# A delta-rule stage: GpSimd's arithmetic on VectorE, shorter taps, one queue for a ring of loads

## The chip, the cores and the metric

The kernel runs as one launch on one core of a Trainium2 chip. The metric is the device time of the launch in microseconds; the time given is the median of three runs. Names of engines: TensorE (PE in the profile, its weight loads PEld), VectorE (DVE), ScalarE (ACT), GpSimd (POOL), SyncE (SP). A q behind a name (SPq) is the queue of instructions of that engine, from which it also issues its DMAs.

## What is computed

The reference is two transformer blocks in float32 on 256 latent tokens of width 1024, with 256 context tokens beside them in the first block. The first block has a mixer of two linear-attention branches and a mixture of 32 experts; the second has dilated and latent attention and a gated feed-forward part. The change lies in the first branch of the first mixer, the gated delta rule. Its q, k and v are projections that pass a depthwise convolution of three by three taps: the latent tokens are an image of 4 rows by 64 columns, the context a single line.

```python
def depthwise_conv2d(img, w):
    return lax.conv_general_dilated(img, w[:, :, None, :], window_strides=(1, 1), padding='SAME', ...)

def conv_latent(t, conv_w):      # rows = 256 // 64 = 4
    return depthwise_conv2d(t.reshape(b, rows, GRID_W, ch), conv_w).reshape(b, l, ch)

def conv_context(t, conv_w):     # the middle row of taps alone
    return depthwise_conv2d(t[:, None], conv_w[mid:mid + 1])[:, 0]

def gated_delta_chunked(q, k, v, g, beta, s0):
    ...
    qg = q * jnp.exp(g)[..., None]
    ...
```

The conditioning of the first block is `silu(c) @ w_mod + b_mod`, six vectors of 1024.

## The kernel before

`build` runs the stages in this order: `pre` (norm, the first third of the conditioning), `gates`, `gdn` (the delta rule), `gla` (the second branch), `merge`, `moe` (the experts' weights as one stream of loads on SP's queue) and `post` (the second block).

The delta rule works on 8 heads in 4 pairs. `gdn_pair` (L391) first loads six weight tiles of a pair from `w_in` on GpSimd's queue (L399). For each head and each of q, k, v it splits the weight into a high and a low part (`wsplit` L381, `split` L48): ScalarE writes the high part `whi` (L49), and VectorE, or the engine handed in, the low part `wlo` (L50). In the first two pairs the split of v (j == 2) is handed to GpSimd. TensorE makes the projection in three products (`mm3`, L76 to L78) into a bank `pj`.

`conv_silu` (L357) then does the convolution with 128 channels on the partitions. ScalarE copies the latent tokens into `padl`, a tile of 6 rows by 66 columns whose outer ring stays zero (L364), writes the middle tap into `acc` (L365) and copies the context into `padc` (L367). Eight further taps are added to the 4 by 64 latent tokens on VectorE, each one instruction over 256 elements (L372). For k and v, which have context tokens, the two outer taps of the middle row are applied in two steps: ScalarE scales a shifted copy into `cx` (L374), GpSimd adds it to `acc` (L375). ScalarE makes the Tanh `th` (L377) and VectorE the final product (L378). q has 256 tokens, k and v 512 each. That is 24 convolutions, 16 of them with context.

TensorE transposes kT (L424), norms follow (L433, L435), and the pair's matrices are made: GpSimd masks a broadcast of the gates, `e` (affine_select, L481), ScalarE takes Exp (L485), VectorE forms `mt` and `at` (L487, L489), ScalarE writes Exp of the gates into `qg` (L490), and GpSimd multiplies that with qT (L491), 16 times in all. The small blocks of `mt` go through scratch memory on SP's queue: `blkD` (L496), `X` (L501); VectorE solves them in 62 dependent steps (L515, L516); the results come back through `solD` (L521, L522) and `AB` (L527, L529), also on SP's queue. `gdn_levels` and `gdn_scan` follow on TensorE.

`gdn` (L650) places the next pair's preparation before the levels and scan of the present one, and between pairs puts filling work: projections of the output gates (`lat_act`, `tok_proj`), and the second and third group of the conditioning, `mod_steps(1)` and `mod_steps(2)`. One step of `mod_steps` (L149) takes two tiles of 128 by 1024 of `w_mod` from the ring on SP's queue (L161), and TensorE multiplies them (L162). After the eighth step GpSimd clears a tile, loads the bias (L167, L170) and stores the sum (L174). Step group 0 runs in `pre`.

All these weights come through one ring of six tiles of 4 KB per partition, `K.ring` (L104), named `w`: 48 loads of `w_mod` on SP's queue, those of `w_in` on GpSimd's (L399, L754, L767). A load waits until the tile that it takes over has been read.

The source names the engine of every instruction. The order within an engine is fixed when the program is built, by a planner that works with estimated costs, and it isn't the order of the source: in the profile, filling work of the first pass stands among the preparation of the second pair. At run time each engine and each queue goes through its instructions in that order and waits on semaphores.

Of the kernel before, what the change touches and what calls it, by code (L numbers as in the profile page):

```python
# [7 lines left out]
F32 = mybir.dt.float32  # L8
# [3 lines left out]
AF = mybir.ActivationFunctionType  # L12
OP = mybir.AluOpType
PSUM = bass.MemoryType.PSUM
DRAM = bass.MemoryType.DRAM
P = 128
# [80 lines left out]
def pre(K, dbg=None):  # L97
    tc, nc, I = K.tc, K.nc, K.I
# [50 lines left out]
    def mod_steps(g):  # L149


        hold = {}

        def step(k):
            if k == 0:
                hold["ps"] = K.psum.tile([P, 512], F32, name="mod", bufs=1)
            ps = hold["ps"]
            for q in range(4):
                if q % 2 == 0:
                    w = ring.tile([P, 1024], F32, name="w")  # L160
                    nc.sync.dma_start(w, I["w_mod"][0, k * P:(k + 1) * P, g * 2048 + q * 512:g * 2048 + (q + 2) * 512])  # L161
                nc.tensor.matmul(ps[32 * q:32 * q + 32, :], csP[:, k, :], w[:, q % 2 * 512:(q % 2 + 1) * 512],  # L162
                                 start=(k == 0), stop=(k == 7), skip_group_check=True)
            if k < 7:
                return
            brow = K.ring.tile([P, 512], F32, name="w") if g else K.wsp.tile([P, 512], F32, name="la", bufs=2)
            nc.gpsimd.memset(brow, 0.0)  # L167
            bm = I["b_mod"][0, g * 2048:(g + 1) * 2048].rearrange("(q n) -> q n", n=512)
            for r in range(2 if g == 0 else 1):
                nc.gpsimd.dma_start(brow[r:P:32, :], bm)  # L170
            row = brow
            nc.vector.tensor_add(row, ps, brow)
            if g:
                nc.gpsimd.dma_start(K.modD[g - 1].rearrange("(q n) -> q n", n=512), row[0:P:32, :])  # L174
                return
            pt = G()
            for b in range(4):
                nc.tensor.transpose(pt[:, b * P:(b + 1) * P], row[:, b * P:(b + 1) * P], K.ident)
            for r in range(2):
                nc.vector.tensor_copy(K.modT[:, r].rearrange("p h (q b) -> p (h q) b", b=4),  # L180
                                      pt.rearrange("p (b q r) -> p r q b", b=4, r=32)[:, r])
        return [lambda k=k: step(k) for k in range(8)]


# [46 lines left out]
def gates(K, dbg=None):  # L231
# [4 lines left out]
    K.gdn_es = ExitStack()  # L236
    padp = K.gdn_es.enter_context(tc.tile_pool(name="pads", reuse_waits="tile", bufs=1, side="right"))
    for i in range(2):
        pl_ = padp.tile([P, 6, 66], F32, name=f"padl{i}")
        pc_ = padp.tile([P, 258], F32, name=f"padc{i}")  # L240
        nc.vector.memset(pl_, 0.0)
        nc.vector.memset(pc_, 0.0)
        K.pads.append((pl_, pc_))
# [113 lines left out]
def conv_silu(K, src, n_tok, ct, out, eng):  # L357

    nc = K.nc
    pl, pc = K.pads[K.npad % 2]  # L360
    K.npad += 1
    acc = K.gpool.tile([P, 512], F32, name="acc", bufs=2)
    al = acc[:, 0:256].rearrange("p (r w) -> p r w", r=4)
    nc.scalar.activation(pl[:, 1:5, 1:65], src[:, 0:256].rearrange("p (r w) -> p r w", r=4), AF.Copy)  # L364
    nc.scalar.activation(acc[:, :n_tok], src, AF.Copy, scale=K.taps[:, 4 * 24 + ct:4 * 24 + ct + 1])  # L365
    if n_tok > 256:
        nc.scalar.activation(pc[:, 1:257], src[:, 256:512], AF.Copy)  # L367
    cx = K.gpool.tile([P, 256], F32, name="cx")
    for tap in (0, 1, 2, 3, 5, 6, 7, 8):
        dy, dx = tap // 3, tap % 3  # L370
        w = K.taps[:, tap * 24 + ct:tap * 24 + ct + 1]
        eng.scalar_tensor_tensor(al, pl[:, dy:dy + 4, dx:dx + 64], w, al, op0=OP.mult, op1=OP.add)  # L372
        if n_tok > 256 and dy == 1:
            nc.scalar.activation(cx, pc[:, dx:dx + 256], AF.Copy, scale=w)  # L374
            nc.gpsimd.tensor_add(acc[:, 256:512], acc[:, 256:512], cx)  # L375
    th = K.gpool.tile([P, 512], F32, name="th", bufs=2)
    nc.scalar.activation(th[:, :n_tok], acc[:, :n_tok], AF.Tanh, scale=0.5)  # L377
    eng.scalar_tensor_tensor(out, th[:, :n_tok], 1.0, acc[:, :n_tok], op0=OP.add, op1=OP.mult)  # L378
# [12 lines left out]
def gdn_pair(K, pr):  # L391
# [14 lines left out]
    for hh in range(2):  # L406
# [5 lines left out]
        H.kT = gp.tile([P, 512], F32, name="kT", bufs=4)  # L412
        vT = gp.tile([P, 512], F32, name="vT", bufs=1)
        for j, (dst, n) in enumerate(((H.qT, 256), (H.kT, 512), (vT, 512))):

            hi, lo = wsplit(K, ws[hh * 3 + j], P, nc.gpsimd if pr < 2 and j == 2 else None)
            ps = psum.tile([P, 512], F32, name="pj", bufs=2)
            for k in range(8):
                mm3(nc, ps[:, :n], hi[:, k, :], lo[:, k, :], K.hh[:, k, :n], K.hl[:, k, :n], k == 0, k == 7)
            conv_silu(K, ps[:, :n], n, j * 8 + h, dst, nc.vector)  # L420
# [40 lines left out]
    for hh, H in enumerate(heads):  # L461
        h = H.h

        pg = K.G()
        for t in range(4):
            nc.tensor.matmul(pg[:, t * P:(t + 1) * P], H.kT[:, t * P:(t + 1) * P], H.kT[:, t * P:(t + 1) * P],
                             start=(t == 0), stop=(t == 3), skip_group_check=True)
        pq = K.G()
        for t in range(2):
            nc.tensor.matmul(pq[:, t * P:(t + 1) * P], H.kT[:, t * P:(t + 1) * P], H.qT[:, t * P:(t + 1) * P],  # L470
                             start=(t == 0), stop=(t == 1), skip_group_check=True)
        H.at = gp.tile([P, 2, 2, P], F32, name="at", bufs=4)
        H.qg = gp.tile([P, 2, 2, P], F32, name="qg", bufs=4)
        H.mt = mt[:, hh]
        H.mt2 = mt
        for d in range(2):
            gbc = gp.tile([P, 4, P], F32, name="gbc", bufs=2)
            nc.scalar.dma_start(gbc, dap(K.gD, d * 32 * P + h * P, [[0, P], [8 * P, 4], [1, P]]))
            e = gp.tile([P, 4, P], F32, name="e", bufs=2)
            s = 1 if d == 0 else -1  # L480
            nc.gpsimd.affine_select(out=e, in_=gbc, pattern=[[0, 4], [s, P]], compare_op=OP.is_ge,  # L481
                                    fill=-1e30, base=0, channel_multiplier=-s)
            for t in range(4):
                col = d * 32 + t * 8 + h
                nc.scalar.activation(e[:, t, :], e[:, t, :], AF.Exp, bias=K.ngc[:, col:col + 1])  # L485
            for t in range(4):
                nc.vector.scalar_tensor_tensor(H.mt[:, d, t, :], pg[:, t * P:(t + 1) * P], H.d[:, d, t:t + 1],  # L487
                                               e[:, t, :], op0=OP.mult, op1=OP.mult)
            nc.vector.tensor_mul(H.at[:, d], pq[:, 0:256].rearrange("p (t i) -> p t i", t=2), e[:, 0:2, :])  # L489
            nc.scalar.activation(H.qg[:, d], gbc[:, 0:2, :], AF.Exp)  # L490
            nc.gpsimd.tensor_mul(H.qg[:, d], H.qg[:, d], H.qT.rearrange("p (t i) -> p t i", t=2))  # L491
    yield


# [1517 lines left out]
```

## Time and profile before

| what | value |
|---|---|
| time, median of 3 runs | 2084.25 us (2083.65 to 2087.07) |
| the profiled execution's own time | 2083.65 us |
| its span, first to last instruction | 2081.9 us |
| TensorE busy | 1898.8 us (91%) |
| VectorE busy | 965.6 us (46%) |
| ScalarE busy | 652.5 us (31%) |
| GpSimd busy | 184.0 us (9%) |
| mean granted clock of TensorE | 0.954 of full speed |

The delta rule runs from about 60 to 560 us, the expert stream from about 740 to 1700 us. "Busy" is the time in which an engine carries out instructions; waiting and issuing DMAs aren't in it, except that a DMA issued by GpSimd counts as busy time of that engine. A wait is listed with the engine that waited, the line that it waited to run, and the instruction or DMA that ended the wait. The granted clock is the mean share of full speed that TensorE was granted in a stretch, between its two levels of 1.2 and 2.4 GHz.

### The profile page before, as it was taken

To read this page: it belongs to the slowest core of one execution; us is meant where nothing else is said; L and a number is where in the kernel's file an instruction comes from. 1 tells how busy PE (TensorE), PEld (TensorE's weight loads), DVE (VectorE), ACT (ScalarE), POOL (GpSimd) and SP (SyncE) were. 2 spreads that over 40 slices of the span, in tenths; PEclk is the share of its full clock that TensorE was granted. 3 is DMA by queue.
4 is the path that set the end of the run, shared out by engine and by line. 5 is a ranking of instruction groups with operands and counts; after the bars stand their busy time and mean duration, and the time that the engine had idled before them with its cause. 6 is when DMAs were issued, how large, how long until landed. Compare 5 with 4: busy or idle time off the path is not lost. (4 is left out here: it accounts for less than half of the span.)

```text
span 2081.9 us, 27700 instructions
## 1 busy us (share of the span) xinstructions
PE 1898.8 (91%) x10742; PEld 1159.6 (56%) x10743; DVE 965.6 (46%) x2245; ACT 652.5 (31%) x1369; POOL 184.0 (9%) x247
## 2 busy tenths in 40 slices
PE   4796989799998999999999999999999889989998
PEld 1664768687986763333333333333333228779997
DVE  2797785857464641212122221221211137676777
ACT  2553545467554420000000000000000004555554
POOL 1343122211112000000000000000000000000000
PEclk8798999899999989999999999999999988998999
DMA  7347654437544689999999999999999994433551
GB/s 261 77 122 206 183 169 116 112 103 206 169 151 151 254 325 417 417 414 418 417 416 418 418 416 417 418 416 417 418 418 416 417 345 139 140 102 121 183 182 41
DMA packets 191939, 569.60 MB, mean 274 GB/s; under 512 B 47919, under 2 KB 90776, under 8 KB 158650
## 3 DMA queue, kind: packets, MB, share of 16 engines
q1 hardware_dynamic: 160064, 507.19, 63.1%
q0 software_dynamic: 13392, 47.72, 7.4%
q10 hardware_dynamic: 18346, 12.86, 2.5%
q8 instruction: 86, 1.41, 0.3%
q14 instruction: 51, 0.42, 0.1%
HBM read 555.22 MB, written 12.50 MB: 273 GB/s over the span
## 5 line engine op out<-in xcount | busy, mean ns | idle before, releaser
L50 DVE TENSOR_TENSOR wlo<-w,whi 128x1024 fp32r<-128x1024 f32 (+1 forms) x185 | 223.9, 1211 | 132.6 <-ACT whi L49 129.8
L1308 PE MATMUL pg<-w,xT 128*64 128x512 f32 x1024 | 274.4, 605 | 3.5 <-DMA w<-in_w_gu_dram 3.4
L1308 PE MATMUL pl<-w,xT 128*64 128x512 f32 x1024 | 268.1, 593 | 0.0
L49 ACT ACTIVATE whi<-w 128x1024 fp32r<-128x1024 f32 (+1 forms) x189 | 197.3, 1047 | 217.8 <-PE pj L77 70.4
L1330 PE MATMUL po<-w,aT 128*64 128x512 f32 x1024 | 239.9, 608 | 7.1 <-DMA w<-in_w_down_dram 5.7
L1230 ACT ACTIVATE th<-ga 128x512 f32<-128x512 f32 x32 | 20.2, 632 | 613.8 <-DVE ga L1228 613.8
L1338 DVE TENSOR_TENSOR o<-po,g 64x512 f32<-64x512 f32 x64 | 44.1, 689 | 260.1 <-PE po L1330 259.4
L1308 PEld LDWEIGHTS pl<-w,xT 128*64 128x64 f32 x1024 | 75.2, 137 | 146.4 <-issue 146.4
L1330 PEld LDWEIGHTS po<-w,aT 128*64 128x64 f32 x1024 | 69.5, 139 | 141.7 <-issue 121.9
L1308 PEld LDWEIGHTS pg<-w,xT 128*64 128x64 f32 x1024 | 65.2, 136 | 139.4 <-issue 115.9
L1228 DVE TENSOR_SCALAR ga<-pg 128x512 f32<-128x512 f32 x32 | 22.1, 691 | 244.8 <-PE pg L1308 244.8
L77 PE MATMUL pj<-wlo,hh 128*128 128x256 f32 x384 | 116.2, 303 | 2.8 <-DVE wlo L50 2.8
L76 PE MATMUL pj<-whi,hh 128*128 128x256 f32 x384 | 115.2, 300 | 2.9 <-ACT whi L49 2.9
L78 PE MATMUL pj<-whi,hl 128*128 128x256 f32 x384 | 114.6, 299 | 0.0
L76 PE MATMUL pj<-hh,whi 128*128 128x512 f32 (+1 forms) x264 | 100.9, 384 | 12.6 <-ACT hh L49 9.1
L372 DVE SCALAR_TENSOR_TENSOR acc<-padl,taps,acc 128x256 f32<-128x256 f32 x192 | 104.3, 557 | 10.1 <-ACT acc L365 8.0
L78 PE MATMUL pj<-hh,wlo 128*128 128x512 f32 (+1 forms) x264 | 100.0, 380 | 5.9 <-DVE wlo L50 5.7
L77 PE MATMUL pj<-hl,whi 128*128 128x512 f32 (+1 forms) x264 | 100.9, 382 | 0.1
L1288 POOL CAST se<-sel 128x128 fp32r<-128x128 f32 x32 | 22.4, 702 | 828.4 <-PE pl L1292 828.4
L1267 PEld LDWEIGHTS tr<-S,h 128*128 128x128 f32 x480 | 57.9, 191 | 48.6 <-issue 34.9
L77 PEld LDWEIGHTS pj<-wlo,hh 128*128 128x128 f32 x384 | 78.0, 203 | 11.0 <-DVE wlo L50 4.2
L1360 PE MATMUL y<-o,PwT 128*128 128x512 f32 (+1 forms) x136 | 72.2, 641 | 13.0 <-DVE o L1338 10.2
(682 smaller groups left out, 3601.7 us busy)
## 6 DMA issues: line engine op xcount, KB each, us to landing
w<-in_w_gu_dram SPq DMA_DIRECT2D x256, 1024.0 KB, 18.2
w<-in_w_down_dram SPq DMA_DIRECT2D x139, 1024.0 KB, 20.0
w<-in_w_in_dram POOLq DMA_DIRECT2D x72, 512.0 KB, 5.4
w<-in_w_mod_dram SPq DMA_DIRECT2D x48, 512.0 KB, 6.9
w<-in_w_up_dram SPq DMA_DIRECT2D x22, 1024.0 KB, 5.1
w<-in_w_in_dram SPq DMA_DIRECT2D x8, 1024.0 KB, 9.8
gbc<-gD ACTq DMA_DIRECT2D x16, 256.0 KB, 6.2
actD<-la ACTq DMA_DIRECT2D x16, 256.0 KB, 5.0
```

Of the source, the lines that this page charges most:

```text
L49: K.nc.scalar.activation(hi, src, AF.Copy)
L50: (lo_eng or K.nc.vector).tensor_sub(lo, src, hi)
L76: nc.tensor.matmul(out, ah, bh, start=first, stop=False, **kw)
L77: nc.tensor.matmul(out, ah, bl, start=False, stop=False, **kw)
L78: nc.tensor.matmul(out, al, bh, start=False, stop=last, **kw)
L372: eng.scalar_tensor_tensor(al, pl[:, dy:dy + 4, dx:dx + 64], w, al, op0=OP.mult, op1=OP.add)
L1267: nc.tensor.matmul(p[:, kk * P:kk * P + m * CAP], h2[:, t, k * P:(k + 1) * P], S[:, t, e0:e1].rearrange("p e c -> p (e c)"), start=(kk == ...
L1288: nc.gpsimd.tensor_copy(se, sel[:, e, :, None].to_broadcast([P, 2, CAP]))
L1308: nc.tensor.matmul(pp[hs, :], xT[:, k, :], w[:, off + half * 512:off + half * 512 + 512], start=False, stop=(k == 7), skip_group_check=True)
L1330: nc.tensor.matmul(po[dh * CAP:(dh + 1) * CAP, :], aT[:, k % 4, (k // 4) * CAP:(k // 4 + 1) * CAP], w[:, kk * 1024 + dh * 512:kk * 1024 + ...
L1338: nc.vector.tensor_mul(outs[e // 2][e % 2 * CAP:(e % 2 + 1) * CAP, dh * 512:(dh + 1) * 512], po[hs], K.g2[hs])
L1360: nc.tensor.matmul(ps[dh], PwT[g][hs, t, :], outs[g][hs, dh * 512:(dh + 1) * 512], start=(g > 0), stop=True)
```

## The change

Five edits. The w_mod loads of groups 1 and 2 are issued from GpSimd's queue; group 0 stays on SP's. The low half of every weight split is made by VectorE. A tap with dy 0 or 2 runs over the three output rows that have a neighbour in the image, and `padl` loses the two outer rows that it no longer needs. The two outer taps of the context are one VectorE instruction each, as those of the latent tokens are, and `cx` goes. The product of `qg` and qT moves to VectorE. The masks (L481) and the issue of the DMAs stay on GpSimd.

```diff
@@ -158,7 +158,7 @@
             for q in range(4):
                 if q % 2 == 0:
                     w = ring.tile([P, 1024], F32, name="w")
-                    nc.sync.dma_start(w, I["w_mod"][0, k * P:(k + 1) * P, g * 2048 + q * 512:g * 2048 + (q + 2) * 512])
+                    (nc.gpsimd if g else nc.sync).dma_start(w, I["w_mod"][0, k * P:(k + 1) * P, g * 2048 + q * 512:g * 2048 + (q + 2) * 512])
                 nc.tensor.matmul(ps[32 * q:32 * q + 32, :], csP[:, k, :], w[:, q % 2 * 512:(q % 2 + 1) * 512],
                                  start=(k == 0), stop=(k == 7), skip_group_check=True)
             if k < 7:
@@ -236,7 +236,7 @@
     K.gdn_es = ExitStack()
     padp = K.gdn_es.enter_context(tc.tile_pool(name="pads", reuse_waits="tile", bufs=1, side="right"))
     for i in range(2):
-        pl_ = padp.tile([P, 6, 66], F32, name=f"padl{i}")
+        pl_ = padp.tile([P, 4, 66], F32, name=f"padl{i}")
         pc_ = padp.tile([P, 258], F32, name=f"padc{i}")
         nc.vector.memset(pl_, 0.0)
         nc.vector.memset(pc_, 0.0)
@@ -361,18 +361,19 @@
     K.npad += 1
     acc = K.gpool.tile([P, 512], F32, name="acc", bufs=2)
     al = acc[:, 0:256].rearrange("p (r w) -> p r w", r=4)
-    nc.scalar.activation(pl[:, 1:5, 1:65], src[:, 0:256].rearrange("p (r w) -> p r w", r=4), AF.Copy)
+    nc.scalar.activation(pl[:, :, 1:65], src[:, 0:256].rearrange("p (r w) -> p r w", r=4), AF.Copy)
     nc.scalar.activation(acc[:, :n_tok], src, AF.Copy, scale=K.taps[:, 4 * 24 + ct:4 * 24 + ct + 1])
     if n_tok > 256:
         nc.scalar.activation(pc[:, 1:257], src[:, 256:512], AF.Copy)
-    cx = K.gpool.tile([P, 256], F32, name="cx")
     for tap in (0, 1, 2, 3, 5, 6, 7, 8):
         dy, dx = tap // 3, tap % 3
         w = K.taps[:, tap * 24 + ct:tap * 24 + ct + 1]
-        eng.scalar_tensor_tensor(al, pl[:, dy:dy + 4, dx:dx + 64], w, al, op0=OP.mult, op1=OP.add)
+
+        r0, r1 = (1, 0, 0)[dy], (4, 4, 3)[dy]
+        eng.scalar_tensor_tensor(al[:, r0:r1], pl[:, r0 + dy - 1:r1 + dy - 1, dx:dx + 64], w, al[:, r0:r1], op0=OP.mult,
+                                 op1=OP.add)
         if n_tok > 256 and dy == 1:
-            nc.scalar.activation(cx, pc[:, dx:dx + 256], AF.Copy, scale=w)
-            nc.gpsimd.tensor_add(acc[:, 256:512], acc[:, 256:512], cx)
+            eng.scalar_tensor_tensor(acc[:, 256:512], pc[:, dx:dx + 256], w, acc[:, 256:512], op0=OP.mult, op1=OP.add)
     th = K.gpool.tile([P, 512], F32, name="th", bufs=2)
     nc.scalar.activation(th[:, :n_tok], acc[:, :n_tok], AF.Tanh, scale=0.5)
     eng.scalar_tensor_tensor(out, th[:, :n_tok], 1.0, acc[:, :n_tok], op0=OP.add, op1=OP.mult)
@@ -412,8 +413,7 @@
         H.kT = gp.tile([P, 512], F32, name="kT", bufs=4)
         vT = gp.tile([P, 512], F32, name="vT", bufs=1)
         for j, (dst, n) in enumerate(((H.qT, 256), (H.kT, 512), (vT, 512))):
-
-            hi, lo = wsplit(K, ws[hh * 3 + j], P, nc.gpsimd if pr < 2 and j == 2 else None)
+            hi, lo = wsplit(K, ws[hh * 3 + j], P)
             ps = psum.tile([P, 512], F32, name="pj", bufs=2)
             for k in range(8):
                 mm3(nc, ps[:, :n], hi[:, k, :], lo[:, k, :], K.hh[:, k, :n], K.hl[:, k, :n], k == 0, k == 7)
@@ -488,7 +488,7 @@
                                                e[:, t, :], op0=OP.mult, op1=OP.mult)
             nc.vector.tensor_mul(H.at[:, d], pq[:, 0:256].rearrange("p (t i) -> p t i", t=2), e[:, 0:2, :])
             nc.scalar.activation(H.qg[:, d], gbc[:, 0:2, :], AF.Exp)
-            nc.gpsimd.tensor_mul(H.qg[:, d], H.qg[:, d], H.qT.rearrange("p (t i) -> p t i", t=2))
+            nc.vector.tensor_mul(H.qg[:, d], H.qg[:, d], H.qT.rearrange("p (t i) -> p t i", t=2))
     yield
 
 
```

## Rows read from the trace of the kernel before

**Rows 1.** Busy us and instructions by stretch: PE, PEld, DVE, ACT, POOL, clock, DMA, GB/s.

```profile
60.00:560.00 500.00, 434.26 (x3365) 358.75 (x3364) 359.58 (x949) 275.79 (x629) 126.56 (x147) 0.90 0.52 142
740.00:1700.00 960.00, 907.47 (x4063) 336.77 (x4060) 204.25 (x378) 68.78 (x125) 22.36 (x31) 0.99 1.01 412
```

**Rows 2.** Waits of TensorE, 60 to 560 us: us, times, longest.

```profile
PE mod L162 <- DMA w<-in_w_mod_dram: 23.3, 7, 8.3
PE g L424 <- DVE kT L378: 10.2, 4, 3.9
PE g L435 <- ACT th L433: 6.5, 3, 2.5
...
PE pj L78 <- POOL wlo L50: 0.2, 1, 0.2
```

**Rows 3.** The source view of L378: ns least, median, most; idle before it.

```profile
L378 DVE SCALAR_TENSOR_TENSOR qT<-th,acc x8: 412/426/969, 88.3 to 380.2; 128x256 f32<-128x256 f32 x8
L378 DVE SCALAR_TENSOR_TENSOR kT<-th,acc x8: 627/688/1074, 89.5 to 397.5; 128x512 f32<-128x512 f32 x8
...
  ACT th L377: 14.0, 7
```

**Rows 4.** The source view of L372, the latent taps.

```profile
L372 DVE SCALAR_TENSOR_TENSOR acc<-padl,taps,acc x192: 468/484/2619, 77.3 to 405.5; 128x256 f32<-128x256 f32 x192
```

**Rows 5.** Groups by line and form, VectorE, 57 to 560 us: busy us, mean ns.

```profile
L372 DVE SCALAR_TENSOR_TENSOR acc<-padl,taps,acc 128x256 f32<-128x256 f32 x192 | 104.3, 557 | 10.1 <-ACT acc L365 8.0
L50 DVE TENSOR_TENSOR wlo<-w,whi 128x1024 fp32r<-128x1024 f32 x58 | 71.2, 1228 | 36.9 <-ACT whi L49 36.9
...
L378 DVE SCALAR_TENSOR_TENSOR qT<-th,acc 128x256 f32<-128x256 f32 x8 | 4.5, 557 | 10.0 <-ACT th L377 10.0
```

**Rows 6.** Groups by line and form, GpSimd, the whole span.

```profile
L375 POOL TENSOR_TENSOR acc<-acc,cx 128x256 f32<-128x256 f32 x32 | 27.9, 872 | 80.9 <-ACT cx L374 76.9 <-DVE acc L372 4.0
...
L399 POOL DMA_DIRECT2D w<-in_w_in_dram x24 | 21.6, 900 | 78.4 <-PE mod L162 42.6 <-DVE taps L255 13.0 <-DVE sc L209 7.5
L491 POOL TENSOR_TENSOR qg<-qg,qT 128x256 f32<-128x256 f32 x16 | 15.2, 954 | 16.2 <-ACT qg L490 13.4 <-DVE qT L378 2.3 <-DVE r L58 0.4
L50 POOL TENSOR_TENSOR wlo<-w,whi 128x1024 fp32r<-128x1024 f32 x4 | 12.3, 3070 | 6.4 <-ACT whi L49 6.2
...
L997 POOL DMA_DIRECT2D gt<-actD x2 | 1.1, 547 | 0.0
```

**Rows 7.** The source view of L843, a product of two tiles.

```profile
L843 DVE TENSOR_TENSOR qg<-qg,qkv x8: 411/418/424, 558.1 to 640.2; 128x256 f32<-128x256 f32 x8
```

**Rows 8.** The source view of L374, the context copies.

```profile
L374 ACT ACTIVATE cx<-padc,taps x32: 492/509/546, 78.8 to 401.4; 128x256 f32<-128x256 f32 x32
```

**Rows 9.** The timeline, 83 to 90 us: start, duration, instruction.

```profile
82.78 2.18 DVE L372 SCALAR_TENSOR_TENSOR acc<-padl,taps,acc 128x256 f32<-128x256 f32 x5
...
85.64 0.73 POOL L375 TENSOR_TENSOR acc<-acc,cx 128x256 f32<-128x256 f32 x1 [0.18 <-ACT cx L374]
...
87.86 0.40 ACT L377 ACTIVATE th<-acc 128x256 f32<-128x256 f32 x1
...
88.29 0.42 DVE L378 SCALAR_TENSOR_TENSOR qT<-th,acc 128x256 f32<-128x256 f32 x1 [3.33 <-ACT th L377]
```

**Rows 10.** The timeline of GpSimd, 137 to 143 us.

```profile
138.22 4.70 POOL L50 TENSOR_TENSOR wlo<-w,whi 128x1024 fp32r<-128x1024 f32 x1 [4.87 <-ACT whi L49]
```

**Rows 11.** Waits of SP's queue, 60 to 420 us: us, times, longest.

```profile
SPq L161 <- PE mod L162: 58.3, 13, 15.0
```

**Rows 12.** The source view of L161, the loads of w_mod.

```profile
L161 SPq DMA_DIRECT2D w<-in_w_mod_dram x48: 327/328/2576, 6.6 to 292.3; - x48
...
DMA to landing us min/median/max: 4.5/6.9/7.9
```

**Rows 13.** The source view of L399, the loads of w_in.

```profile
L399 POOL DMA_DIRECT2D w<-in_w_in_dram x24: 882/892/949, 31.7 to 314.0; - x24
...
DMA to landing us min/median/max: 4.5/6.6/11.5
```

## The prediction, made before the changed kernel was run

> **What bounds the kernel now.** I read the engine times by stretch first. From 740 to 1700 us the expert weights stream in with the DMA engines full (share 1.01, 412 GB/s): nothing in the delta-rule stage can make that stretch shorter, it can only let it begin earlier. The change lies before it, from about 60 to 560 us. There TensorE is busy 434.3 of 500 us, VectorE 359.6, ScalarE 275.8, GpSimd 126.6, at a mean granted clock of 0.90 [rows 1]. So TensorE is the nearest thing to a bound, and what a change in this stretch can give is its idle time, 65.7 us, and some of the clock that is not granted. Next I read what ends TensorE's waits: the conditioning weights (mod, L162) 23.3 us in 7 waits; kT of the convolution (L424) 10.2 in 4; the Tanh-side tile th (L435) 6.5 in 3; GpSimd's own wlo only 0.2 [rows 2]. Two of these the change touches: the convolution's chain (VectorE, ScalarE and GpSimd in turn) and the loads of w_mod.
>
> After 560 us nothing is changed. TensorE's work up to the stream follows in order on the shared buffers, and the stream's loads wait for buffers that this work frees, so I pass a shift at 560 us on to the end whole; if the stream's start did not follow, every number below would shrink towards no change.
>
> **The change part by part.** Busy time of VectorE first.
>
> Taps with dy 0 and 2 lose one row of four: 6 taps in each of 24 convolutions, 144 instructions, 64 elements less. The same operation at 256 and 512 elements takes 426 and 688 ns [rows 3], 1.02 ns per element, so 65 ns each: -9.4 us. Bounds: 0 (if the cost were all fixed) and a quarter of 484 ns [rows 4], -17.4.
>
> The context taps: 32 new instructions of 256 elements, at the 484 ns of the present tap [rows 4]: +15.5 us; at 426 ns [rows 3] 13.6. They lie between the last latent tap and Tanh, so they lengthen a convolution's VectorE part, by 0.97 less 0.39 us.
>
> The weight splits of v in the first two pairs: 4 at 1228 ns [rows 5] in place of 3070 on GpSimd [rows 6]: +4.9 us. The query scaling: 16 multiplies of the very shape that L843 does in 418 ns [rows 7]: +6.7 us. GpSimd loses 27.9 + 15.2 + 12.3 = 55.4 us [rows 6], ScalarE the 32 copies of 509 ns, 16.3 us [rows 8].
>
> Given back is the stretching. The tap's median is 484 ns but its mean 557, its longest 2619 [rows 4, 5]: 192 x 73 = 14.0 us; qT's final instruction has 426 against 557, 8 x 131 = 1.0 [rows 3, 5]. Nothing in a tap's size varies, so I lay the tail to GpSimd's arithmetic beside it. Bounds: 0 back (it is something else) and the 15.0 us whole; I take the whole, because the median is far below the mean, which a few collisions explain and a general slowness does not. Short instructions are probably stretched too; I leave them out.
>
> Sum for VectorE: -9.4 + 15.5 + 4.9 + 6.7 - 15.0 = +2.7 us. At its share of 72% I put **+2 us** on the path.
>
> Now the waits. The tail of a convolution: in the first head VectorE's last tap ends at 84.96, but ScalarE still has a context copy to make, GpSimd's add ends at 86.37, th starts at 87.86 and qT at 88.29 [rows 9]. With all taps on VectorE, th can start when they end. VectorE waits 14.0 us in 7 times for th [rows 3], and TensorE 16.7 us in 7 for kT and th together [rows 2]. Part of this is Tanh's own duration, and the new taps come before it; I take half of VectorE's 14.0: **-7 us**. Bounds 0 and -14.0.
>
> The split on GpSimd: one of the four runs 138.22 to 142.92 [rows 10], with adds and the next mask behind it on that queue. Four splits last 12.3 us there and 4.9 on VectorE; 7.4 less, of which TensorE feels little directly (0.2, [rows 2]). I take **-3 us**, bounds 0 and -7.4.
>
> The shared queue. 32 of the 48 loads of w_mod (those of the second and third group) go from SP's queue to GpSimd's, where the ring's other loads, the masks (affine_select), brow's memset and the bias loads are. What each costs GpSimd is not in the trace; the nearest rows are 547 ns (a load of 4 KB rows, L997) and 900 ns (L399, 512-byte rows) [rows 6]: 17.5 to 28.8 us; I take the first, as w_mod's rows are of 4 KB. It is less than the 55.4 us freed, so GpSimd stays mostly idle and this is hidden; were that cover gone, masks and loads would be late by it. What stands behind a load that waits for its buffer: masks, whose reader is ScalarE's Exp, and the w_in loads, whose readers are the splits. What is gained: w_in loads no longer stand behind adds that wait for ScalarE, and the small SP transfers (blkD, X, solD, AB) no longer behind w_mod. Most waits of these loads on SP are for TensorE to free a buffer, 58.3 us in 13 [rows 11], and no queue changes that: there are six buffers. To landing both kinds of queue take about the same, 6.9 and 6.6 us median [rows 12, 13]. So of the 23.3 us I take **-4**, bounds -23.3 (all gone) and +23.3 (doubled by what is queued ahead).
>
> GpSimd's loads beside a busy VectorE: the 24 issues of L399 last 882 to 949 ns, in a stretch where VectorE is busy 72% [rows 1, 13]. That is even; I see no load held up by VectorE at its issue. The Trainium skill, "SBUF — State Buffer", section "SBUF: two separate sides", says otherwise: loads issued by GpSimd starve while VectorE holds the port pair that the two share, and it puts 620 ns alone against some 3100 ns beside a copy. By that figure 32 loads would be later by an estimated 79 us in all, in place of nothing.
>
> The clock. 0.10 of 500 us is not granted [rows 1], 50 us. About 14 of 65.7 us of idle time go; in proportion that would be 10 us, but TensorE's own idle time is in the 50 and the level also falls elsewhere: **-3 us**, bounds 0 and -10.
>
> Costed at nothing: the smaller pad's memset (two, at the start of gates, with VectorE idle afterwards).
>
> **Sum**: +2 - 7 - 3 - 4 - 3 = -15 us. The profiled execution's own time is 2083.65 us (span 2081.9 and 1.75 around it), so 2068.65; the median of the runs, 2084.25, lies 0.6 above it: **2069 us**. What a measurement of this kernel can tell from no change is 0.2%, 4.2 us.
>
> **The rivals.**
> - All seven waits for w_mod go: -23.3 in place of -4, **2050 us**. For it: w_in loads now stand behind arithmetic on GpSimd, in the same ring. Against: the waits on a freed buffer. Chance 0.10.
> - TensorE covers it: what VectorE and ScalarE gain is taken up because TensorE is busy 87% and its order is fixed; only the two or three largest stalls move, **2082 us**. Chance 0.10.
> - The stretching is not GpSimd's: then the new 17.7 us of VectorE stay, all on the path in its full stretches, +17.7 for +2, which eats the rest: **2085 us**. Against it stands the tail of [rows 4]. Chance 0.04.
> - Head of the queue (slower): on one in-order queue a w_mod load that waits for TensorE holds the masks and the w_in loads behind it; the 58.3 us of such waits were SP's, where little stood behind them. TensorE's waits double: +23.3 for -4, a sum of +12, **2096 us**. It decides once the 13 waits average over the slack of what is behind; at 4.5 us each that is close. Against it: the ring's loads queue in the order in which buffers free. Chance 0.12.
> - Starved loads (slower): each of the 7 waits grows by the difference between the slowest landing on GpSimd's queue and the median on SP's, 11.5 - 6.9 = 4.6 us [rows 12, 13]: +32 for -4, +21, **2105 us**. The even issues speak against it. Chance 0.06. The Trainium skill's section named above is the rule by which it would happen.
>
> **How the numbers follow.** My forecast has 0.58; with the first rival 0.68 for faster. The two near no change give 0.14, the two slower ones 0.18. The range is 2046 to 2088 us: it takes in the first rival and the bounds of the tail, split and clock terms, and leaves out the slower rivals (0.18) and little else.
>
> **What would show it.** The groups by line: taps of two sizes, about 484 and 420 ns, with mean equal to median; no GpSimd arithmetic but masks; 32 loads of w_mod on GpSimd at some 0.55 us. TensorE's idle time from 60 to 560 us some 15 us less, with shorter waits L424 and L435, and the stream's first full slice as much earlier. Wrong: TensorE's waits for w_mod above 23.3 us, masks or w_in late behind a waiting load, a VectorE that is busy over 375 us in the stretch, or a shift at 560 us that the stream swallows.

## The result, and the profile after

The changed kernel takes **2102.51 us** (median of 4 runs, 2098.03 to 2104.36) against 2085.59 (4 runs of the kernel before on the same chip): a ratio of **1.0075, 95% interval 1.0061 to 1.0090**, 15.6 us slower by the ratio (the two medians are 16.9 us apart). Forecast were 2069 us, a range up to 2088, and 0.68 for faster. Its profiled execution has a span of 2101.6 us, 19.7 more than before.

First the stretches, in the columns of [rows 1]:

```profile
60.00:560.00 500.00, 418.59 (x3212) 341.65 (x3211) 331.79 (x980) 251.73 (x575) 89.42 (x119) 0.87 0.50 138
740.00:1700.00 960.00, 909.47 (x4091) 348.62 (x4089) 215.06 (x391) 78.10 (x139) 22.85 (x33) 0.99 1.00 409
```

In the delta rule every engine has become less busy, TensorE too, by 15.7 us, and its granted clock is lower (0.87 for 0.90, nearer to the lower of its two levels). Less work is done in the same 500 us: all engines wait more. TensorE's idle time was to fall by some 15 us; it rose by 15.7, from 65.7 to 81.4. The stream runs as it did.

Then the groups of VectorE and of GpSimd that the change touches, as in [rows 5] and [rows 6]:

```profile
L50 DVE TENSOR_TENSOR wlo<-w,whi 128x1024 fp32r<-128x1024 f32 x60 | 74.1, 1236 | 61.7 <-ACT whi L49 57.6 <-PE pj L78 4.0
L373 DVE SCALAR_TENSOR_TENSOR acc<-padl,taps,acc 128x192 f32<-128x192 f32 x144 | 58.1, 413 | 9.7 <-ACT acc L365 9.1
L373 DVE SCALAR_TENSOR_TENSOR acc<-padl,taps,acc 128x256 f32<-128x256 f32 x48 | 23.0, 480 | 0.2
L376 DVE SCALAR_TENSOR_TENSOR acc<-padc,taps,acc 128x256 f32<-128x256 f32 x32 | 15.3, 479 | 0.0
L491 DVE TENSOR_TENSOR qg<-qg,qT 128x256 f32<-128x256 f32 x16 | 6.8, 423 | 0.0
```

```profile
L161 POOL DMA_DIRECT2D w<-in_w_mod_dram x32 | 17.2, 538 | 104.2 <-PE mod L162 49.4 <-DVE wlo L50 24.0 <-DVE S L642 12.2
```

The prices are those of the forecast: taps of two sizes at 413 and 480 ns, with no tail left (L373, the former L372, has a longest of 490 ns where [rows 4] has 2619), context taps at 479, products at 423, 32 loads at 538. VectorE's idle time ahead of `wlo` is up instead: 61.7 us, for 36.9 in [rows 5].

The waits of TensorE from 60 to 560 us, as in [rows 2]:

```profile
PE mod L162 <- DMA w<-in_w_mod_dram: 16.4, 8, 5.6
PE pj L78 <- DVE wlo L50: 13.9, 3, 11.3
PE sc L556 <- DMA AB<-solD: 11.1, 2, 7.3
PE sc L556 <- DMA gbc<-gD: 9.7, 1, 9.7
PE pj L77 <- DVE wlo L50: 6.8, 4, 3.1
PE g L424 <- DVE kT L379: 6.5, 3, 3.2
PE pj L76 <- ACT whi L49: 3.2, 4, 1.3
PE pj L76 <- ACT padc L367: 3.1, 1, 3.1
PE pj L76 <- ACT acc L365: 2.9, 1, 2.9
```

The waits that the forecast wanted shorter are shorter: `w_mod` 16.4 us for 23.3, `kT` 6.5 for 10.2, and `th`, 6.5 before, is below these rows. Others have come up: 20.7 us for `wlo` (L77 and L78), and 20.8 us at L556, where the levels of a pair begin. Before, these were 8.5 and 5.0:

```profile
PE pj L78 <- DVE wlo L50: 5.7, 1, 5.7
PE sc L556 <- DMA AB<-solD: 5.0, 4, 3.5
PE pj L77 <- DVE wlo L50: 2.8, 3, 1.7
```

At L556 the profile puts 9.7 us down to `gbc`, a broadcast of the gates. L556 doesn't read that tile (its operands are `AB` and `mt`), so this releaser is in doubt; reads of the solve's result `AB` were still being issued when that wait ended at 323.1 us.

How far each kernel has got is best read at the first load of the expert weights. Up to there, from 60 us, the stretch view gives (before ends at 676.7 us, the changed kernel at 700.5):

```profile
60.00:676.70 616.70, 543.20 (x4060) 449.96 (x4059) 431.49 (x1153) 338.47 (x814) 144.79 (x184) 0.92 0.51 147
```

```profile
60.00:700.50 640.50, 548.18 (x4039) 451.33 (x4038) 410.31 (x1199) 324.39 (x782) 112.87 (x164) 0.89 0.49 142
```

So 23.8 us are lost before the stream: TensorE idles 92.3 us (640.50 less 548.18) in place of 73.5, 18.8 more, and takes 5.0 us longer for its work at a lower clock. About 4 us come back later. VectorE is 21 us less busy and ScalarE 14, so neither has become a bound by its work.

Where does it go? The first pair's solve ends at 208.3 us, 12.8 us earlier than before (221.1). The second pair's ends at 303.6 us (303.7 before), the third's at 410.0 for 395.5, and the last store of the delta rule's output is issued at 570.2 for 553.7. The first gain is real, and the stretches after it lose it and more. The third pair's solve begins 11.4 us late (363.1 us for 351.7), and some 14 of the 23.8 us come after the fourth solve, which ends at 503.4 for 493.4.

**What the order did.** The planner has laid out all engines anew. Here is one wait of the changed kernel, in its timeline of VectorE, then of TensorE:

```profile
393.55 0.48 DVE L373 SCALAR_TENSOR_TENSOR acc<-padl,taps,acc 128x256 f32<-128x256 f32 x1
393.94 0.38 DVE L516 TENSOR_TENSOR X<-X,xtmp 128x224 f32<-128x224 f32 x1
394.25 0.16 DVE L70 TENSOR_TENSOR rs_a<-r 128x6 f32<-128x6 f32 x1
394.32 0.48 DVE L373 SCALAR_TENSOR_TENSOR acc<-padl,taps,acc 128x256 f32<-128x256 f32 x1
394.72 0.37 DVE L515 TENSOR_TENSOR xtmp<-L,X 128x208 f32<-128x208 f32 x1
...
403.63 0.42 DVE L373 SCALAR_TENSOR_TENSOR acc<-padl,taps,acc 128x192 f32<-128x192 f32 x1
403.96 0.26 DVE L516 TENSOR_TENSOR X<-X,xtmp 128x96 f32<-128x96 f32 x1
404.13 1.23 DVE L50 TENSOR_TENSOR wlo<-w,whi 128x1024 fp32r<-128x1024 f32 x1
405.26 0.24 DVE L515 TENSOR_TENSOR xtmp<-L,X 128x80 f32<-128x80 f32 x1
```

```profile
393.63 0.46 PE L76 MATMUL pj<-whi,hh 128*128 128x256 f32 x1 [1.26 <-ACT whi L49]
405.41 0.80 PE L78 MATMUL pj<-hh,wlo 128*128 128x512 f32 x1 [11.32 <-DVE wlo L50]
```

TensorE stops at 394.09 for a split. VectorE is not idle in these 10 us; it is full, with taps of the next head, norms and steps of the solve, one after another, and the split has its place behind them, ahead of the step of 80 columns. The same split stands ahead of the step of 208 columns in the order of before, 16 steps earlier. That the order is at fault was at this point an idea only; the runs below test it.

### The profile page after: what moved, and what is told of

It reads as the page before. It is cut to its first block, busy times and chain, and to the rows that moved or that the text cites. A ratio compares the mean times of both kernels' runs of the same rounds, so it can differ in the third digit from the quotient of the medians.

```text
span 2101.6 us, 27624 instructions
## 1 busy us (share of the span) xinstructions
PE 1900.6 (90%) x10742; PEld 1160.7 (55%) x10743; DVE 945.6 (45%) x2297; ACT 639.5 (30%) x1337; POOL 152.0 (7%) x227
## 3 DMA queue, kind: packets, MB, share of 16 engines
q1 hardware_dynamic: 155456, 490.41, 60.2%
## 5 line engine op out<-in xcount | busy, mean ns | idle before, releaser
L50 DVE TENSOR_TENSOR wlo<-w,whi 128x1024 fp32r<-128x1024 f32 (+1 forms) x189 | 229.3, 1214 | 164.3 <-ACT whi L49 157.4
L77 PE MATMUL pj<-wlo,hh 128*128 128x256 f32 x384 | 114.9, 299 | 6.8 <-DVE wlo L50 6.8
L78 PE MATMUL pj<-hh,wlo 128*128 128x512 f32 (+1 forms) x264 | 103.4, 393 | 14.2 <-DVE wlo L50 14.2
L78 PE MATMUL pj<-whi,hl 128*128 128x256 f32 x384 | 113.1, 295 | 0.0
L77 PE MATMUL pj<-hl,whi 128*128 128x512 f32 (+1 forms) x264 | 101.7, 385 | 0.1
L1360 PE MATMUL y<-o,PwT 128*128 128x512 f32 (+1 forms) x136 | 71.6, 635 | 14.3 <-DVE o L1338 10.2
L373 DVE SCALAR_TENSOR_TENSOR acc<-padl,taps,acc 128x192 f32<-128x192 f32 (+1 forms) x192 | 79.5, 429 | 9.9 <-ACT acc L365 9.1
L77 PEld LDWEIGHTS pj<-wlo,hh 128*128 128x128 f32 x384 | 77.3, 201 | 10.1 <-DVE wlo L50 8.6
L76 PEld LDWEIGHTS pj<-whi,hh 128*128 128x128 f32 x384 | 76.9, 200 | 9.8 <-ACT whi L49 6.1
```

What stands on the lines that cost most here:

```text
L50: (lo_eng or K.nc.vector).tensor_sub(lo, src, hi)
L76: nc.tensor.matmul(out, ah, bh, start=first, stop=False, **kw)
L77: nc.tensor.matmul(out, ah, bl, start=False, stop=False, **kw)
L78: nc.tensor.matmul(out, al, bh, start=False, stop=last, **kw)
L373: eng.scalar_tensor_tensor(al[:, r0:r1], pl[:, r0 + dy - 1:r1 + dy - 1, dx:dx + 64], w, al[:, r0:r1], op0=OP.mult, op1=OP.add)
L1360: nc.tensor.matmul(ps[dh], PwT[g][hs, t, :], outs[g][hs, dh * 512:(dh + 1) * 512], start=(g > 0), stop=True)
```

## The experiments

The time of the kernel before is 2085.55 to 2087.92 us in the four groups of runs. Each ratio is against the kernel before on the same chip, with its 95% interval.

### One part alone, the rest laid out by the planner

The first theory was that the shared queue costs the time (A), the second that any edit makes the planner choose a new order, which costs it (B), the third that VectorE's added work does (C).

The queue edit alone, on the kernel before:

```diff
-                    nc.sync.dma_start(w, I["w_mod"][...])
+                    (nc.gpsimd if g else nc.sync).dma_start(w, I["w_mod"][...])
```

> The kernel before with the queue edit alone: the 32 loads of w_mod on GpSimd's queue, all else as it was. Theory A (the shared queue costs the time: on SP's queue the loads of w_mod stood in line with the small transfers solD and AB, on GpSimd's they run beside them): some 2100 to 2105 us, and the time from the end of a solve to the first matmul of the levels (L556) grows from 7 to 11 us to 13 us or more. Theory B (any edit that moves costs makes the planner lay out another order, and the loss is what that order happens to bring together): no rule for the time, anything from 2070 to 2105 us; but slow solves-to-levels only where four or more loads of the ring are issued between them. Theory C (VectorE's added work costs the time): 2085 us, no change.

Measured 2096.96 us, 1.0051 (1.0025 to 1.0077): a little below A's range, well above C's, within B's.

The whole change without the queue edit:

```diff
-                    (nc.gpsimd if g else nc.sync).dma_start(w, I["w_mod"][...])
+                    nc.sync.dma_start(w, I["w_mod"][...])
```

> The changed kernel with the loads of w_mod back on SP's queue; taps, splits and products as in the changed kernel. Theory A: the queue's loss is gone and the arithmetic's gain is left, 2066 to 2075 us. Theory B: between 2070 and 2105 us, with waits for AB again wherever ring loads fall beside it. Theory C: 2100 us as the changed kernel.

Measured 2116.10 us, 1.0157 (1.0109 to 1.0205). Slower still: theory A falls, and the time lies above the ranges of B and C as well.

The shorter taps and the smaller pad alone, on the kernel before:

```diff
-        pl_ = padp.tile([P, 6, 66], F32, name=f"padl{i}")
+        pl_ = padp.tile([P, 4, 66], F32, name=f"padl{i}")
...
-        eng.scalar_tensor_tensor(al, pl[:, dy:dy + 4, dx:dx + 64], w, al, op0=OP.mult, op1=OP.add)
+        r0, r1 = (1, 0, 0)[dy], (4, 4, 3)[dy]
+        eng.scalar_tensor_tensor(al[:, r0:r1], pl[:, r0 + dy - 1:r1 + dy - 1, dx:dx + 64], w, al[:, r0:r1], ...)
```

> The kernel before with the shorter taps alone (three rows of four, the smaller pad): nothing but 144 shorter VectorE instructions, some 9.8 us less of VectorE. A theory in which only costs count: 2078 to 2085 us, never slower. Theory B: the order is laid out anew from the first convolution on, so the time can go either way by 10 us or more; a slower time shows that the order alone can cost that much, since no instruction of this kernel costs more than before.

Measured 2103.70 us, 1.0105 (1.0058 to 1.0152). This is the telling one: the program has the same instructions as before, 144 of them shorter, and it loses 16 us.

The context taps, the splits and the products on VectorE, with whole taps and SP's queue:

```diff
-            nc.scalar.activation(cx, pc[:, dx:dx + 256], AF.Copy, scale=w)
-            nc.gpsimd.tensor_add(acc[:, 256:512], acc[:, 256:512], cx)
+            eng.scalar_tensor_tensor(acc[:, 256:512], pc[:, dx:dx + 256], w, acc[:, 256:512], op0=OP.mult, op1=OP.add)
...
-            hi, lo = wsplit(K, ws[hh * 3 + j], P, nc.gpsimd if pr < 2 and j == 2 else None)
+            hi, lo = wsplit(K, ws[hh * 3 + j], P)
...
-            nc.gpsimd.tensor_mul(H.qg[:, d], H.qg[:, d], ...)
+            nc.vector.tensor_mul(H.qg[:, d], H.qg[:, d], ...)
```

> The kernel before with GpSimd's arithmetic on VectorE alone (context taps, four splits, the query products), whole taps, w_mod on SP's queue. VectorE's stretching is gone (mean of a tap 480 ns). Theory C: slower, 2095 us or more, with VectorE busier by some 10 us. Theory A: 2075 to 2083 us. Theory B: either way, by the waits for AB and wlo.

Measured 2121.21 us, 1.0170 (1.0126 to 1.0214). Up to its first load of the expert weights, at 718.5 us, VectorE is 422.6 us busy, less than the 431.5 of before although it has 52 instructions more, so its busy time doesn't explain the loss. The time is in C's range, its reason isn't. Four edits, four slower kernels, and the parts do not add up to the whole: nothing in these times belongs to one edit. That fits B, but does not show it.

### The same instructions, the order held

The next runs hold the order. At the end of the part that the planner lays out in one piece (all up to the experts), each instruction gets an edge to the one ahead of it in a list for its engine. Such an edge fixes the order of issue alone; nothing waits by it. The lists are read from another kernel's program. In short form:

```diff
+def pin(tc, nc):
+    ins = {i.name: i for i in nc.cur_bb.bb.instructions}
+    for names in ORDER:
+        for prev, name in zip(names, names[1:]):
+            tc.add_manual_dep(ins[name], prev, NO_WAIT, reason="pin")
...
+    pin(tc, nc)
     with tc.If(m > CAP):
```

The shorter taps alone, in the order of before:

> The shorter taps and the smaller pad alone, with each engine's instructions held in exactly the order that the kernel before has (an ordering edge between neighbours of each engine's list, no wait). Theory order (the loss is what the newly planned order brings together): the 16 us that this edit lost beside the kernel before go, and of the 9.4 us that the taps save some part is seen: 0 to 9 us faster than before, ratio 0.9955 to 1.000. Theory cost (the shorter taps cost time by themselves, by their shape or their place): it stays some 16 us slower, ratio 1.005 to 1.0105.

Measured 2079.98 us, **0.9973** (0.9955 to 0.9990). The 16 us are gone and 5.7 are gained. (No run holds the kernel before in its own order; that holding an order costs little by itself is seen from this run.) GpSimd's adds still run beside the taps here, and a tap of 256 elements still takes 562 ns on average:

```profile
L374 DVE SCALAR_TENSOR_TENSOR acc<-padl,taps,acc 128x256 f32<-128x256 f32 x48 | 26.9, 562 | 0.5
```

The kernel before, not an instruction changed, in the order that the planner chose for the shorter taps:

> The kernel before with not one instruction changed, but with each engine's instructions held in the order that was planned for the shorter taps. Theory order: it is as slow as that kernel or a little slower, since its taps are longer: 14 to 26 us slower than before, ratio 1.007 to 1.0125. Theory cost: the time of the kernel before, ratio 0.998 to 1.002.

Measured 2107.89 us, **1.0110** (1.0084 to 1.0137). The order alone costs some 23 us. Its stretch up to the first expert load (702.5 us):

```profile
60.00:702.50 642.50, 546.47 (x4017) 451.14 (x4016) 431.92 (x1143) 337.65 (x809) 139.85 (x183) 0.89 0.49 142
```

VectorE, ScalarE and TensorE are as busy as in the kernel before, within 3.3 us, but the stretch is 25.8 us longer. TensorE idles 96.0 us, at a clock of 0.89: in its sums the picture of the changed kernel, without the change. The waits that make it up are others, those for `kT` above all (10.2 us before):

```profile
PE g L424 <- DVE kT L378: 22.8, 6, 7.0
PE mod L162 <- DMA w<-in_w_mod_dram: 12.9, 3, 7.5
PE pj L78 <- DVE wlo L50: 10.8, 4, 5.0
```

The whole change, in the order of before (the planner places only what changed its engine):

> The whole change, with every instruction that the kernel before also has held in the order of before on its engine; the 32 context taps stand right behind the tap ahead of them, and the planner places only the 4 splits, 16 products and 32 loads that changed their engine. Theory order: the terms of the prediction's sum now add up, 8 to 22 us faster than before, ratio 0.9895 to 0.996. Theory cost (VectorE's added work or the shared queue costs the time whatever the order): 8 to 20 us slower, ratio 1.004 to 1.0095.

Measured 2079.71 us, **0.9970** (0.9951 to 0.9990): faster than before, but less so than the range of the order theory (0.9895 to 0.996).

The same, with the loads of w_mod left on SP's queue:

> As the run with the whole change held in the order of before, but with the loads of w_mod left on SP's queue. It tells what the shared queue is worth at a fixed order. Theory order: 4 us slower than that run (the prediction's term), within a bound of 10 either way; both faster than before. Theory cost by the shared queue: this run is some 15 us faster than that one. Theory cost by VectorE's added work: both are slower than before by 8 to 20 us.

Measured 2074.17 us, **0.9939** (0.9918 to 0.9960). Its first load of the expert weights is issued at 669.5 us:

```profile
60.00:669.50 609.50, 538.07 (x4064) 445.22 (x4063) 416.95 (x1207) 325.60 (x784) 89.64 (x132) 0.93 0.52 149
```

All four runs go the way of theory B, though the whole change gains less than it asked for, and is faster without the shared queue, not slower as expected. That an instruction or the queue costs the 16 us whatever the order falls on all four. Between the profiled executions of before and of this last run the stretch is 7.2 us shorter (the medians differ by 11.6): 2.1 us less idle time of TensorE and 5.1 us less for its work, at a clock of 0.93. Its longest waits for the convolution have become shorter than in [rows 2]:

```profile
PE mod L162 <- DMA w<-in_w_mod_dram: 22.4, 6, 9.0
PE g L424 <- DVE kT L379: 7.9, 3, 3.9
PE sc L556 <- DMA AB<-solD: 7.2, 2, 5.2
PE pj L78 <- DVE wlo L50: 5.4, 2, 4.9
PE g L435 <- ACT th L433: 4.9, 2, 2.7
```

### The parts at a fixed order

The queue edit alone, in the order of before:

> The queue edit alone (32 loads of w_mod issued by GpSimd), with all other instructions held in the order of before; the planner places only these loads on GpSimd's queue. Theory: at a fixed order the shared queue costs some 5 us, as the two runs of the whole change with and without it differ (2079.7 and 2074.2), because w_mod loads now wait behind w_in loads and adds: 2 to 9 us slower than before, ratio 1.001 to 1.0045. Rival (the prediction's term was right and that difference is noise): 4 us faster, ratio 0.997 to 0.999.

Measured 2089.61 us, 1.0011 (0.9996 to 1.0025): no gain; the interval reaches from 0.8 us faster to 5.2 us slower.

VectorE's added work alone, in the order of before:

> VectorE's added work alone (context taps, the 4 splits, the 16 products; whole taps, w_mod on SP's queue), with all other instructions held in the order of before. Theory: at a fixed order the edits add up, so with rows alone at -5.7 us and both at -11.5 this one gives some -6: ratio 0.994 to 0.9995. Rival (VectorE's added work costs time, and only the shorter taps pay): 0 to 8 us slower, ratio 1.000 to 1.004.

Measured 2074.59 us, **0.9937** (0.9921 to 0.9953), 13 us faster by the ratio, 11.4 between the medians. I had expected half of it. So the shorter taps, worth 5.7 us by themselves, add nothing once GpSimd's arithmetic is gone (0.9939 with both): I read it so that with GpSimd out of the way VectorE is no longer what those stretches wait for; no run tests that.

### Which engine's order

The whole change, with TensorE's order alone held as before, then SP's and GpSimd's alone, then VectorE's and ScalarE's alone:

```diff
-    for names in ORDER:
+    for names in (ORDER of the engines named):
```

> The whole change, with only TensorE's instructions held in the order of before; the planner lays out all other engines and queues anew around that. If the place of TensorE's filling work is what costs the time, most of the 23 us between the change and its run held in the order of before come back: 2077 to 2088, ratio 0.996 to 1.001. If it is the order on VectorE, ScalarE or the queues, little comes back: 2093 to 2105, ratio 1.0035 to 1.009.

Measured 2091.22 us, 1.0029 (1.0015 to 1.0043): a little under half comes back, between the two ranges.

> The whole change, with only SP's and GpSimd's instructions (the queues from which nearly all loads are issued) held in the order of before; the planner lays out TensorE, VectorE and ScalarE anew around that. If the order in which the ring's loads and the solve's small transfers are issued is what costs the time, most of the 23 us come back: 2077 to 2088, ratio 0.996 to 1.001. If it is the order on the computing engines, little comes back: 2093 to 2105, ratio 1.0035 to 1.009.

Measured 2113.82 us, 1.0124 (1.0107 to 1.0141): nothing comes back; the run is slower than the changed kernel and than both ranges.

> The whole change, with only VectorE's and ScalarE's instructions held in the order of before; the planner lays out TensorE and the queues anew around that. Holding TensorE alone gave back some 10 of the 23 us between the change and its run held whole, holding the queues none. If VectorE's and ScalarE's order carries the rest, this run lies well below the change: 2079 to 2092, ratio 0.997 to 1.003. If no engine's order carries it alone and only the whole layout does, little comes back: 2095 to 2110, ratio 1.0045 to 1.0115.

Measured 2079.39 us, **0.9970** (0.9950 to 0.9989), the same as with everything held. So holding VectorE's and ScalarE's order is enough. It doesn't show that the loss lies in their order alone: the planner laid out TensorE anew, and came out almost where it was before. Matched by line and tiles, TensorE's instructions up to 650 us stand on average 1.7 places from their place in the kernel before, and 26 places in the changed kernel. The run that held TensorE's order alone is the cleaner separation: there VectorE's order was new, and a little over half of the loss stayed. In this last run's timeline of VectorE the late split stands early again:

```profile
383.62 0.39 DVE L516 TENSOR_TENSOR X<-X,xtmp 128x224 f32<-128x224 f32 x1
383.93 0.16 DVE L71 SCALAR_TENSOR_TENSOR rs_a<-rs_a,nq 128x6 f32<-128x6 f32 x1
384.00 1.22 DVE L50 TENSOR_TENSOR wlo<-w,whi 128x1024 fp32r<-128x1024 f32 x1
```

It is made at 384.00, and the longest wait of TensorE for a split between 300 and 410 us is 4.68 us in place of 11.32. The planner of the changed kernel has also put more of the next pair's taps between the steps of a solve: by the timelines 103 other instructions within the second pair's solve and 88 within the third's, where this run has 69 and 74, and the two solves last 53.3 and 46.9 us for 50.8 and 43.8. The solve is a chain of dependent steps, TensorE needs its end, and each tap in between puts that off. The third pair's solve also begins later, at 363.1 us for 353.7. This is no general account of the loss. In the kernel before in the new order, which loses as much, the same two solves hold 64 and 65 other instructions where before has 62 and 66. What the two slow orders share is the late third solve, which begins at 363.6 us there and at 351.7 before. Why it is late in both was not isolated.

## Why the prediction was wrong

**The step that failed** is one that the sum never priced: that all other instructions keep their places. The prediction says of TensorE that "its order is fixed". It is fixed at run time, but it is made when the program is built, by a planner with estimated costs, and the change alters the costs. Every term was read from a trace with one order and added up for a kernel with another. Keeping all else, the new order costs 22 us (1.0075 against 0.9970); on unchanged instructions it was some 23. No rival named it: 2105 us for starved loads is near the result by chance, since those loads were issued evenly and TensorE waited less for them. Nor did the signs of being wrong catch it: the waits for w_mod fell to 16.4 us, VectorE stayed under 375, and the stream did not swallow the shift. What is shown is that the order costs the time. Which of the changed places costs how much is not.

Its terms, against the runs that hold the order:

- **VectorE's sum, +2 us on the path, and the tail of the convolution, -7; split -3; clock -3: -11 in all.** Measured with the queue left alone: 0.9939, some -13. The sum is near by luck, for its parts are not right. Of the 8 us that the first three terms took from TensorE's waits, 2.1 came, and TensorE's own work took 5.1 us less, at a higher clock, where 3 were put. TensorE's waits for `kT` and `th` went from 16.7 to 12.8 us, but VectorE's own wait for `th`, half of which was the -7, did not fall: 14.0 us in 7 before, 16.9 in 9 here. No run has the splits alone. VectorE's busy time was to rise by 2.7 us and fell by 14.5, from 431.49 to 416.95 up to the first expert load. The single durations add up to 4.5 us less, not 2.7 more: small instructions were stretched too, which the sum left out (a solve step of L515 took 336 ns on average before and 316 here). The other 10 us are a fault of the adding: records of neighbouring VectorE instructions overlap, as the five taps of [rows 9] show, which take 2.18 us together and some 484 ns each. A sum of single durations counts the overlap twice.
- **The stretching is GpSimd's**: right. The tap of 256 elements went from a mean of 557 ns to 480, with none over 490, once GpSimd had only masks and DMAs to do, and stayed at 562 where only the taps were shortened. The Trainium skill, "SBUF — State Buffer", section "SBUF: two separate sides", has VectorE and GpSimd lock each other out of a port pair that they share; this trace agrees as far as the tail goes.
- **The shared queue, -4, bounds 23.3 either way**: no gain, and most likely a loss. At a fixed order it comes to some +2 us alone (interval from -0.8 to +5.2) and +5.5 in the whole change (2079.71 for 2074.17; the intervals overlap). With the order held, TensorE's wait for w_mod is 27.3 us on the shared queue and 22.4 on SP's: the direction of the rival of the head of the queue, at a fifth of its size. That it gives nothing because the loads wait for TensorE to free a buffer, as [rows 11] said, fits the rows: from 60 to 420 us they wait for that 56.9 us on GpSimd's queue and 60.2 on SP's. No run tests it.
- **Starved loads**: not seen. All 32 loads were issued within 528 to 564 ns. That section of the Trainium skill has loads issued by GpSimd starve while VectorE runs an instruction in a mode that takes both ports, such as a float32 copy, and reports no such stall beside `tensor_tensor`. No load of this trace shows the stall, and the prediction's 79 us carried a figure for copies over to a stretch of mostly other instructions.
- **The shift passes on whole**: right from the first expert load on, within some 4 us; between 560 us and that load it grew. In the run with SP's queue 7.2 us at the first expert load are 7.2 us at the end (span 2074.7); of the changed kernel's 23.8, 19.7 arrive. At the last store of the delta rule it was 16.5.

What stays open: why the second branch, from the last delta-rule store to the first expert load, takes 130.3 us in the changed kernel and 123.0 before. With the whole order of the delta rule held it is 123.4. Of the 7.3 us TensorE is busy 4.2 longer (748 instructions for 730, at a granted clock of 0.96 for 0.99) and idle 3.1 more. And nearly half of the loss comes back with TensorE's order alone, which says that the orders of the engines hang together, not how.

**Versions that beat both kernels**, all at the order of before: VectorE's added work alone (0.9937), the whole change but the queue (0.9939), the whole change (0.9970, also with VectorE's and ScalarE's order alone held), and the shorter taps alone (0.9973).

## What to carry to other kernels

Where a planner lays out the instructions, an edit of any size can bring a new order, and its effect (here 22 us) can exceed the edit's own (here -13 to +6). Compare the orders of the two programs before believing a time, and hold the order when an edit is to be judged; the run that counts is the unchanged kernel in the new order. If a gain appears only at a fixed order, fix the order in the kernel.

## What the runs showed of the hardware

Taking GpSimd's 55 us of arithmetic to VectorE gave 13 us at a fixed order, although VectorE was the busier engine and took the work over. A tap of 256 elements took 557 ns on average beside it and 480 without.

The solve's small transfers can take very different times to issue. Here are the first three reads of `AB` for the second pair, in the queue of SP of the changed kernel, then of the run in the order of before with SP's queue:

```profile
309.31 4.42 SPq L527 DMA_DIRECT2D AB<-solD  x3
```

```profile
301.72 2.19 SPq L527 DMA_DIRECT2D AB<-solD  x3
```

Loads of the ring were being issued by GpSimd within both: three of w_mod in the first, two of w_in in the second.

```profile
310.91 1.60 POOL L161 DMA_DIRECT2D w<-in_w_mod_dram  x3
```

```profile
303.51 1.76 POOL L400 DMA_DIRECT2D w<-in_w_in_dram  x2 [3.91 <-DMA modD<-w]
```

So this pair of rows doesn't say what slows the first, and no run tries it.
